# A two-block network on one core: x loaded first, the bonus sums in 16 wide products, and layer 1's last four conditioning vectors moved into the dilated attention

## The chip, the core and the metric

One core of one Trainium2 chip runs the whole program in one launch. The metric is the device time of an execution in microseconds. The two kernels are compared by the median of their runs.

## The reference, cut to what matters

All of it is fp32, for one sequence of S = 256 tokens of width D = 1024. The first block has two layers, RWKV-7 mixing (layer 0) and dilated attention (layer 1), each followed by a hierarchical mixture of experts (MoE). Each layer is modulated by six vectors of 1024 that depend on one conditioning vector c alone:

```python
mod = silu(c) @ ada_w[l] + ada_b[l]          # 1024 x 6144, split in six
shift_a, scale_a, gate_a, shift_m, scale_m, gate_m = split(mod, 6)
x = x + gate_a * mixer(modulate(rms_norm(x), shift_a, scale_a))
x = x + gate_m * moe(modulate(rms_norm(x), shift_m, scale_m))
```

The bonus of the RWKV layer is one number for each token, head and direction, which weighs the token's value: `bonus = sum(r * k_dir * r_k, over the head's 64 channels) * v`. A second block with four more mixers (NSA, stick-breaking, convolution, MoBA) and their MLPs follows; the change does not touch it.

## The kernel before, in words

The program is written for a framework that schedules each engine's instructions and inserts the waits. Weights come through a ring of raw slots of 8 KB a partition: `load` (L317) issues a DMA of 1 MB on SP's queue into the next slot, and SP waits there until the slot is free. Most products are made in three parts of a high and a low half: `split` (L332, L333) has ScalarE write wh, the rounded weights, and VectorE write wl, the rest, in groups of four of 128x512; L361 to L363 are the three products. In the RWKV core the ring has two slots, in the dilated attention six.

`Stream` (L112) runs units of three steps (load, product, end) and issues loads ahead; `staged` (L145) and `weave` interleave units of different kinds, the latter by a string with a letter for each step.

**Conditioning.** `Ada` (L2207) makes the vectors. A vector is four units: a unit loads 128x4x512 of `ada_w` and makes four products (L2239) of a 32-column stationary with silu(c) in one column (`cs`) and 512 moving columns, each in its own 32 partitions. After every second unit VectorE adds the result to the table `am` (L2244). `features` (L2258, L2260) turns a vector into columns by eight products with the selector `asel`, `gate` spreads one over the partitions.

**The order of the program.** The body (L2290) first issues the four units of vector 0, then x (L2325), then those of vector 1, all on SP, and the router's weights of layer 0 (L1248 to L1252: seven small DMAs) before the RWKV layer's own. It normalizes x (L433, L2332), transposes it (L464), and makes vectors 0 and 1, their features, and h (L1674) as x modulated. Seven small DMAs on ScalarE's queue bring the parameter vectors (`vecs`, L494, L500). The other 40 units, the rest of both layers, are a stream that `Rwkv` (L1550) uses as filler: 10 units before the core, 30 in it.

**RWKV.** LoRAs (L1666), k and r projection (`project`, L1631), keys, then for each half: decay rates (L1859), `bonus` (L1800) and `scores` (L1921). In `bonus` VectorE makes the products kq (L1812) and TensorE sums them over a head by 64 products of a 128x64 stationary and two moving columns (L1819); VectorE copies the result (L1823). The core (L1964) runs two chains of four steps each, in pieces that take turns. After three of four turns one fill unit is taken: `if n % 4 < 3: next(fill, None)`.

**After it** come the first MoE (weights through the ring as well), `Dilated` (L1124) with 36 blocks of projection weights ("b"), 16 attention units of several steps ("a": scores, turn, outs) and the output projection ("O", "o"), the second MoE and the second block.

Of the kernel before, what the change touches and what calls it, by code (L numbers as in the profile page):

```python
# [136 lines left out]
def take(g, n):  # L137

    for _ in range(n):
        if next(g, STOP) is STOP:  # L140
            return
        yield

# [118 lines left out]
class Net:  # L262
# [195 lines left out]
    def transposed(self, src, each):  # L458

        for k0 in range(0, 8, 2):  # L460
# [5 lines left out]
            each(k0, ps)  # L466
# [657 lines left out]
class Dilated:  # L1124


    def __init__(self, net, pool, X, w_qkv, w_o, dist, ga):
# [80 lines left out]
        weave("b" * 9 + "babbabbabbabb" * 3 + "Oaaoaoaaa", b=Stream(units), a=staged(16, scores, turn, outs),  # L1208
# [337 lines left out]
ROWY = (0, 64)  # L1546
# [3 lines left out]
class Rwkv:  # L1550
# [10 lines left out]
    def __init__(self, net, xT, G, sh, gate, vec, w, filler, x_src, room, more):  # L1561

        self.net, self.nc, self.tc, self.xT = net, net.nc, net.tc, xT
# [65 lines left out]
    def project(self):  # L1631
# [9 lines left out]
        with net.pool("rp1", "right") as p1:  # L1641
# [83 lines left out]
            with net.pool("rwh", "right", bufs=2) as net.whp, net.pool("rwl", "right", bufs=2) as net.wlp, \  # L1725
# [74 lines left out]
    def bonus(self, pk):  # L1800

        net, nc, v = self.net, self.nc, self.v
        psb = net.w()
        rk = pk.tile([128, 8, 2], F32, name="rkh")
        nc.vector.tensor_tensor(rk, v["rk"][:, 0].unsqueeze(2).to_broadcast([128, 8, 2]),
# [158 lines left out]
    def core(self):  # L1964
# [19 lines left out]
        while chains:  # L1984
            for c in list(chains):
# [7 lines left out]
                if n % 4 < 3:  # L1993
                    next(fill, None)
# [212 lines left out]
class Ada:  # L2207

    def __init__(self, net, pool, cvec, ada_w, ada_b):
# [5 lines left out]
        self.sel = pool.tile([128, 32], F32, name="asel")  # L2217
        nc.vector.tensor_reduce(self.sel, net.ident.rearrange("p (k j) -> p j k", k=4), axis=AX.X, op=ALU.add)
        nc.vector.tensor_tensor(self.sel[:, 0:6], self.sel[:, 0:6], net.ident[:, 8:14], op=ALU.add)
        self.m = [pool.tile([128, 2, 512], F32, name=f"am{l}") for l in range(2)]  # L2220
        for l in range(2):
            nc.gpsimd.memset(self.m[l], 0.0)
            nc.scalar.dma_start(self.m[l][8:14], ada_b[l].rearrange("(v a b) -> v a b", v=6, a=2))
# [283 lines left out]
```

## Time and profile before

| | |
|---|---|
| runs | 2543.34, 2545.49, 2546.83 us (median 2545.49) |
| profiled execution | 2545.04 us, span 2543.3 us |
| mean granted TensorE clock | 0.964 |
| TensorE, weight loads, VectorE, ScalarE busy | 2395.5, 1942.3, 1462.3, 1110.1 us |
| DMA | 547.71 MB, mean 215 GB/s |

The stages that the change touches, in us from the span's start: start and LoRAs 0 to 75, k/r projection 75 to 132, rates, bonus and scores 140 to 205, core 247 to 397, first MoE 457 to 710, dilated attention 717 to 1005.

How to read it: busy time is given for each engine, and a busy TensorE is not TensorE at its peak. An idle stretch counts only if what comes after it is late; so the waits and what ended them matter more than the busy shares. PEclk is the granted TensorE clock as a share of full speed. In the trace an fp32 product has two rows, so that "x8" under TensorE are four products.

### The profile page before, as it was taken

How to read it: one execution, taken by the hardware profiler on the slowest of the kernel's cores; microseconds unless marked ns; L12 is line 12 of the kernel's file. 1: busy time of each engine (PE TensorE's matmuls, PEld its weight loads, DVE VectorE, ACT ScalarE, POOL GpSimd, SP SyncE). 2: the span in 40 equal slices, each digit the busy share in tenths (PEclk: the TensorE clock that was granted, in tenths of full speed). 3: DMA queues.
4: the chain of work that ended last, by engine and by line, in shares of the span. 5: the costliest groups of instructions: out<-in, count | busy, mean ns of one | idle time of the engine just before them, and what ended most of it. 6: DMA issues, size and time to landing. Idle time of an engine off the chain costs nothing. (4 is left out here: it accounts for less than half of the span.)

```text
span 2543.3 us, 41711 instructions
## 1 busy us (share of the span) xinstructions
PE 2395.5 (94%) x17098; PEld 1942.3 (76%) x17098; DVE 1462.3 (57%) x2879; ACT 1110.1 (44%) x2259; POOL 92.3 (4%) x111
## 2 busy tenths in 40 slices
PE   6987888999989999899988999999999899999999
PEld 3855555665579998665557899898999789987998
DVE  4878765443255554433267655566557865577654
ACT  3634233221155553311144544555446654455553
POOL 0000000000000000000022000000000000011000
PEclk9978988999999999899999999999999999999999
DMA  9375888799845444799945255544554245554552
GB/s 309 117 281 199 286 276 318 287 419 412 325 158 173 144 149 156 290 420 400 356 137 195 97 185 182 183 165 149 183 184 147 67 149 182 182 182 133 172 185 74
DMA packets 234077, 547.71 MB, mean 215 GB/s; under 512 B 24810, under 2 KB 75010, under 8 KB 207118
## 3 DMA queue, kind: packets, MB, share of 16 engines
q1 hardware_dynamic: 230774, 532.70, 58.9%
q0 software_dynamic: 1424, 9.44, 1.0%
q8 instruction: 138, 2.26, 0.4%
q10 hardware_dynamic: 1672, 2.74, 0.3%
q14 instruction: 69, 0.57, 0.1%
HBM read 534.36 MB, written 10.49 MB: 214 GB/s over the span
## 5 line engine op out<-in xcount | busy, mean ns | idle before, releaser
L333 DVE TENSOR_TENSOR wl<-raw,wh 128x512 fp32r<-128x512 f32 (+1 forms) x944 | 605.9, 690 | 407.3 <-ACT wh L332 406.2
L332 ACT ACTIVATE wh<-raw 128x512 fp32r<-128x512 f32 (+1 forms) x944 | 530.7, 621 | 506.2 <-issue 214.7
L361 PE MATMUL wk<-xh,wh 128*128 128x256 f32 x1664 | 469.6, 283 | 1.4 <-ACT xh L470 1.3
L362 PE MATMUL wk<-xl,wh 128*128 128x256 f32 x1664 | 469.9, 283 | 0.2 <-DVE xl L472 0.2
L363 PE MATMUL wk<-xh,wl 128*128 128x256 f32 x1664 | 469.7, 283 | 0.0
L361 PEld LDWEIGHTS wk<-xh,wh 128*128 128x128 f32 x1664 | 313.6, 189 | 4.5 <-ACT xh L470 3.0
L362 PEld LDWEIGHTS wk<-xl,wh 128*128 128x128 f32 x1664 | 313.1, 188 | 2.1 <-DVE xl L472 0.5
L363 PEld LDWEIGHTS wk<-xh,wl 128*128 128x128 f32 x1664 | 313.6, 189 | 0.3 <-DVE wl L333 0.3
L1466 PE MATMUL wk<-raw,xg 128*64 128x256 f32 x2048 | 229.4, 381 | 0.0
L1466 PEld LDWEIGHTS wk<-raw,xg 128*64 128x64 f32 x2048 | 144.8, 137 | 80.5 <-issue 11.1
L362 PE MATMUL wk<-wl,hh 128*128 128x512 f32 x512 | 201.4, 393 | 0.0
L361 PE MATMUL wk<-wh,hh 128*128 128x512 f32 x512 | 200.9, 392 | 0.0
L363 PE MATMUL wk<-wh,hl 128*128 128x512 f32 x512 | 199.1, 389 | 0.0
L1472 DVE SCALAR_TENSOR_TENSOR hid<-sg,gs,wk 128x256 f32<-128x256 f32 x32 | 21.4, 668 | 232.1 <-ACT sg L1470 232.1
L1493 PE MATMUL wk<-raw,hidT 128*64 128x512 f32 x512 | 148.4, 598 | 0.0
L361 PE MATMUL wk<-wh,xh 128*128 128x256 f32 (+2 forms) x416 | 141.6, 342 | 1.5 <-ACT xh L470 1.5
L362 PE MATMUL wk<-wl,xh 128*128 128x256 f32 (+2 forms) x416 | 139.3, 335 | 1.7 <-DVE wl L333 1.7
L363 PE MATMUL wk<-wh,xl 128*128 128x256 f32 (+2 forms) x416 | 138.7, 335 | 0.0
L1470 ACT ACTIVATE sg<-wk 128x256 f32<-128x256 f32 x32 | 12.3, 384 | 279.9 <-PE wk L1466 279.9
L363 PEld LDWEIGHTS wk<-wh,hl 128*128 128x128 f32 x512 | 96.1, 188 | 21.7
L361 PEld LDWEIGHTS wk<-wh,hh 128*128 128x128 f32 x512 | 96.2, 188 | 20.9
L362 PEld LDWEIGHTS wk<-wl,hh 128*128 128x128 f32 x512 | 96.2, 188 | 18.6
(491 smaller groups left out, 3873.2 us busy)
## 6 DMA issues: line engine op xcount, KB each, us to landing
raw<-in_moe_w_gate_dram SPq DMA_DIRECT2D x64, 1024.0 KB, 9.4
raw<-in_moe_w_up_dram SPq DMA_DIRECT2D x64, 1024.0 KB, 8.8
raw<-in_moe_w_down_dram SPq DMA_DIRECT2D x64, 1024.0 KB, 8.9
raw<-in_mlp_w_up_dram SPq DMA_DIRECT2D x64, 1024.0 KB, 5.4
raw<-in_mlp_w_down_dram SPq DMA_DIRECT2D x64, 1024.0 KB, 5.2
raw<-in_ada_w_dram SPq DMA_DIRECT2D x45, 1024.0 KB, 7.7
raw<-in_at_w_qkv_dram SPq DMA_DIRECT2D x36, 1024.0 KB, 5.1
raw<-in_sb_w_in_dram SPq DMA_DIRECT2D x12, 1024.0 KB, 5.1
```

Source lines behind the costliest of these rows:

```text
L332: nc.scalar.activation(wh[:, s], raw[:, s], AF.Copy)
L333: self.next_low().tensor_tensor(wl[:, s], raw[:, s], wh[:, s].bitcast(F32), op=ALU.subtract)
L361: mm(out, lh, rh, start=start, stop=False, skip_group_check=True)
L362: mm(out, lh, rl, start=False, stop=False, skip_group_check=True)
L363: mm(out, ll, rh, start=False, stop=stop, skip_group_check=True)
L1466: mm(ps[e * 64:e * 64 + 64, half * 256:half * 256 + 256], xg[:, k, (2 * j + e) * 64:(2 * j + e) * 64 + 64], wts[2 * half + e][:, k], start ...
L1470: nc.scalar.activation(s, ps[:, 0:256], AF.Silu)
L1472: nc.vector.scalar_tensor_tensor(h.rearrange("p f c -> p c f"), s.rearrange("p (c f) -> p c f", f=2), gs, ps[:, 256:512].rearrange("p (c f ...
L1493: mm(ps[e * 64:e * 64 + 64, :], hT[:, f * 128 + e * 64:f * 128 + e * 64 + 64], wts[e][:, f, c * 512:c * 512 + 512], start=f == 0, stop=f = ...
```

## The change

It has four parts. (1) x is loaded by ScalarE's queue as its first DMA; its transposes are made in two pairs between conditioning units, the parameter vectors after them; the router's weights are loaded from within `project`. (2) A conditioning unit loads 128x2x1024 (rows of 4 KB instead of 2 KB); its four products lie in the same 32-partition groups as before, but the two halves of a vector now stand in different partitions of `am`, 512 columns wide; vectors 0 and 1 are added once each. `features` for the MoE (`emod`) has 16 products instead of 8. (3) The bonus takes 16 products with 16 stationary and 256 moving columns, then two ScalarE copies and four transposes. (4) The core's filler holds 24 units instead of 40 and is taken at one turn in three. Vectors 2 to 5 of layer 1 are loaded in `Dilated`, as a stream of 16 units ("m" in the weave); VectorE multiplies them by silu(c) and adds up (`sums`: 64 operations of 128x512), TensorE sums each over the partitions by two products of a one-column selector.

```diff
@@ the body's start
+                nc.scalar.dma_start(x, x_src)
                 nc.sync.dma_start(cst, flat(I['c']).rearrange("(a b) -> a b", b=128))
...
-                    first += [(lambda w=load(): w, prod, end) for load, prod, end in ada.units(0, v)]
-                    if v == 0:
-                        nc.sync.dma_start(x, x_src)
+                    first += [(lambda w=load(): w, prod, end) for load, prod, end in ada.units(0, v, 4)]
...
-                for _ in range(4):
+                for _ in range(3):
                     next(first)
...
-                net.transposed(xn, lambda k0, ps: xT.append((k0, ps)))
+                ts = net.transposes(xn)
+                xT += take2(ts, 2)
+                for _ in range(2):
+                    next(first)
+                xT += take2(ts, 2)
+                next(vecs)
                 trace(first)
-                next(vecs)
...
-            rest = [u for l in range(2) for v in range(2 - 2 * l, 6) for u in rest(l, v)]
-            rest = Stream(rest, 0)
+            fill = Stream([u for l in range(2) for v in range(2 - 2 * l, 6 - 4 * l) for u in rest(l, v)], 0)
...
-            routers.append(weights(0, nc.sync))
...
-            Rwkv(net, xT, scale(0, 0), shift(0, 0), lambda p: ada.gate(p, 0, 2), vec, w, rest, x_src, room, more)
+            Rwkv(net, xT, scale(0, 0), shift(0, 0), lambda p: ada.gate(p, 0, 2), vec, w, fill, x_src, room, more,
+                 lambda: routers.append(weights(0, nc.sync)))
@@ project
                     net.fetch(t, w["rkv"][0], [key])
+                self.later()
@@ bonus
-            for c in range(4):
-                s = c if d == 0 else 3 - c
-                nc.tensor.matmul(psb[ROWY[d]:ROWY[d] + 64, s * 16 + 2 * p:s * 16 + 2 * p + 2],
-                                 q[:, c * 64:c * 64 + 64], rk[:, p], start=(p == 0 and c == 0), stop=True,
-                                 skip_group_check=True)
+            nc.tensor.matmul(psb[:16, d], rk[:, 16 * p:16 * p + 16], q, start=i == 0, stop=p == 7, skip_group_check=True)
         yield from staged(16, product, sums, gap=2)
-        nc.vector.tensor_copy(self.bon, psb[:, :64].rearrange("p (s h) -> p s h", s=4))
+        bt = pk.tile([16, 4, 2, 64], F32, name="bt")
+        for d in range(2):
+            nc.scalar.activation(bt[:, ::1 - 2 * d, d], psb[:16, d].rearrange("p (c t) -> p c t", c=4), AF.Copy)
+        yield
+        ps = net.w()
+        for s in range(4):
+            nc.tensor.transpose(ps[:, s * 16:s * 16 + 16], bt[:, s].rearrange("p d t -> p (d t)"), net.ident[:16, :16])
+        nc.vector.tensor_copy(self.bon, ps[:, :64].rearrange("p (s h) -> p s h", s=4))
@@ core
-                if n % 4 < 3:
+                if n % 3 == 0:
                     next(fill, None)
@@ Dilated
-        weave("b" * 9 + "babbabbabbabb" * 3 + "Oaaoaoaaa", b=Stream(units), a=staged(16, scores, turn, outs),
+        weave("M" + "bbm" * 4 + "b" + "babbmabbmabbabbm" * 3 + "mmmOaaoaoaaa", m=more, b=Stream(units), a=staged(16, scores, turn, outs),
@@ Ada, new
+    def sums(self, pool, l, v):
...
+            def prod(raw):
+                if i == 0:
+                    t.extend(pool.tile([128, 512], F32, name="og", bufs=2) for _ in range(2))
+                for k in range(2):
+                    c = self.cs[:, 2 * i + k, 31:32]
+                    for h in range(2):
+                        r = raw[:, k, h * 512:h * 512 + 512]
+                        if i + k == 0:
+                            nc.vector.tensor_scalar(t[h], r, c, None, op0=ALU.mult)
+                        else:
+                            nc.vector.scalar_tensor_tensor(t[h], r, c, t[h], op0=ALU.mult, op1=ALU.add)
+
+            def end():
+                if i == 3:
+                    ps = net.w()
+                    for h in range(2):
+                        nc.tensor.matmul(ps[32 * h:32 * h + 32], self.one[:, 31 - v:63 - v], t[h],
+                                         start=True, stop=True, skip_group_check=True)
+                    nc.vector.tensor_tensor(self.m[l][0:64], self.m[l][0:64], ps[0:64], op=ALU.add)
```

Where instructions move, three places. First SP's queue at the start of the program (x, raw: the slots that the loads land in), before:

```order
L317 DMA raw<-in_ada_w_dram 128x4x512 x4
L2325 DMA x<-in_x_dram 128x2x1024
L317 DMA raw<-in_ada_w_dram 128x4x512 x4
L1248 DMA rw<-in_moe_router_g_dram 128x8x4
L1250 DMA rw<-in_moe_router_e_dram 128x8x8 x4
...
L1658 DMA x<-in_rw_w_dram 128x8x64 x2
```

and in the changed program:

```order
L322 DMA raw<-in_ada_w_dram 128x2x1024 x8
L1669 DMA x<-in_rw_w_dram 128x8x64 x2
...
L361 DMA raw<-in_rw_w_rkv_dram 128x4x512
L1258 DMA rw<-in_moe_router_g_dram 128x8x4
L1260 DMA rw<-in_moe_router_e_dram 128x8x8 x2
```

x is gone from this queue (it stands first on ScalarE's), and the router's loads stand behind those of the LoRAs and among those of the r weights.

Second, TensorE at the bonus (rkh, kq: its operands; lw: rates; AR, BK: scores; raw, cs: conditioning), before:

```order
L1819 MATMUL wk<-rkh,kq 64x2 x8
L1859 MATMUL wk<-cpack,lw_246 128x128
L1819 MATMUL wk<-rkh,kq 64x2 x4
...
L2239 MATMUL wk<-raw,cs 32x512
L1819 MATMUL wk<-rkh,kq 64x2 x4
L2239 MATMUL wk<-raw,cs 32x512 x3
```

and in the changed program:

```order
L1832 MATMUL wk<-kq,rkh 16x256 x14
L1840 MATMUL wk<-cpack,bt 128x16 x4
L1877 MATMUL wk<-cpack,lw_237 128x128 x4
L2265 MATMUL wk<-raw,cs 32x512 x4
L1877 MATMUL wk<-cpack,lw_238 128x128 x4
L2265 MATMUL wk<-raw,cs 32x512 x4
```

The bonus products stand together, the rate products and the conditioning groups come whole behind them.

Third, VectorE in the dilated attention of the changed program, after its first blocks (og: the running sums of a vector; wl: the splits; dz, dst: an attention step), where before there stood only rows of wl, dz and dst:

```order
L2293 TENSOR_SCALAR og<-raw,cs 128x512 x2
L2295 SCALAR_TENSOR_TENSOR og<-raw,cs,og 128x512 x5
L338 TENSOR_TENSOR wl<-raw,wh 128x512 x4
L2295 SCALAR_TENSOR_TENSOR og<-raw,cs,og 128x512
L338 TENSOR_TENSOR wl<-raw,wh 128x512
L1175 SCALAR_TENSOR_TENSOR dz<-dist,wk 128x256 x3
L338 TENSOR_TENSOR wl<-raw,wh 128x512
L1180 TENSOR_REDUCE dst<-dz 128x1
L338 TENSOR_TENSOR wl<-raw,wh 128x512 x2
L1182 RECIPROCAL dst<-dst 128x1
```

The sums stand before and between the splits of the next weights, one to five in a row.

## Rows read from the trace of the kernel before

**Rows 1.** The page's part 1: busy us, share of the span, instructions.
```profile
PE 2395.5 (94%) x17098; PEld 1942.3 (76%) x17098; DVE 1462.3 (57%) x2879; ACT 1110.1 (44%) x2259; POOL 92.3 (4%) x111
```
**Rows 2.** Windows, start: length, busy us by engine, PEclk, DMA share, GB/s.
```profile
24.00:28.00 4.00, 4.00 (x20) 3.05 (x22) 0.21 (x1) 0.00 (x0) 0.00 (x0) 1.00 1.05 388
28.00:32.00 4.00, 4.00 (x33) 1.59 (x25) 1.14 (x3) 0.00 (x0) 0.00 (x0) 1.00 0.76 86
36.00:40.00 4.00, 0.00 (x0) 0.03 (x1) 3.32 (x8) 3.98 (x9) 0.00 (x0) 0.54 1.14 237
```
**Rows 3.** TensorE's timeline, start: at, us, instructions, [idle before <-releaser].
```profile
23.70 3.65 PE L464 MATMUL wk<-cpack,xn 128*128 128x128 f32 x16 [5.15 <-DVE xn L2332]
27.27 3.84 PE L2239 MATMUL wk<-raw,cs 128*32 128x512 f32 x24
...
32.12 1.06 PE L2239 MATMUL wk<-raw,cs 128*32 128x512 f32 x8
34.00 1.05 PE L2258 MATMUL wk<-asel,am 128*128 128x2 f32 x8 [0.81 <-DVE am L2244]
40.00 1.19 PE L1666 MATMUL wk<-xs,x 128*128 128x256 f32 x2 [4.95 <-DMA w2p<-in_rw_w_dram]
```
**Rows 4.** VectorE's timeline of the start, the same columns.
```profile
22.80 1.42 DVE L2332 TENSOR_SCALAR xn<-x,rstd 128x1024 f32<-128x1024 f32 x2 [0.89 <-POOL rstd L419]
...
33.26 0.69 DVE L2244 TENSOR_TENSOR am<-am,wk 128x512 f32<-128x512 f32 x1 [1.36 <-PE wk L2239]
...
37.54 0.69 DVE L1679 SCALAR_TENSOR_TENSOR xx<-xx,h 128x512 f32<-128x512 f32 x1
```
**Rows 5.** ScalarE's timeline of the start.
```profile
19.16 0.63 ACT L433 ACTIVATE xn<-x 128x512 f32<-128x512 f32 x1 [10.37 <-DMA x<-in_x_dram]
...
35.56 3.76 ACT L1674 ACTIVATE h<-wk,mods 128x256 f32<-128x256 f32 x8 [13.85 <-DVE mods L2351]
```
**Rows 6.** SP's DMA issues of the start (timeline).
```profile
18.32 2.55 SPq L1248 DMA_DIRECT2D rw<-in_moe_router_g_dram  x1
...
32.17 1.00 SPq L1658 DMA_DIRECT2D x<-in_rw_w_dram  x2
```
**Rows 7.** TensorE's groups, 155-182 us: | busy us, mean ns | idle before.
```profile
L1819 PE MATMUL wk<-rkh,kq 128*64 128x2 f32 x128 | 12.1, 234 | 0.6 <-DVE kq L1812 0.6
L2239 PE MATMUL wk<-raw,cs 128*32 128x512 f32 x16 | 7.7, 1060 | 0.0
```
**Rows 8.** Line L1819, bonus products: who waited for it (us, times).
```profile
  DVE kq L1812: 12.0, 6
```
**Rows 9.** Window of the bonus.
```profile
164.00:172.00 8.00, 8.00 (x44) 5.22 (x44) 1.28 (x3) 2.92 (x6) 0.00 (x0) 0.50 0.99 373
```
**Rows 10.** TensorE's costliest group in the core, 236-400 us.
```profile
L2239 PE MATMUL wk<-raw,cs 128*32 128x512 f32 x240 | 41.0, 689 | 15.3 <-DMA raw<-in_ada_w_dram 14.0 <-ACT oT L2183 1.4
```
**Rows 11.** Line L2239, 230-400 us: who waited for it (us, times).
```profile
  DVE am L2244: 27.2, 9
```
**Rows 12.** Windows of k/r projection, core, first MoE and dilated attention.
```profile
80.00:100.00 20.00, 20.00 (x166) 20.00 (x165) 13.65 (x29) 11.21 (x21) 0.00 (x0) 0.98 0.00 1
275.00:320.00 45.00, 38.24 (x752) 25.16 (x750) 32.14 (x84) 13.72 (x30) 2.15 (x4) 0.96 0.96 319
520.00:560.00 40.00, 40.00 (x288) 25.05 (x286) 15.72 (x29) 8.83 (x18) 0.00 (x0) 1.00 1.01 418
760.00:800.00 40.00, 40.00 (x334) 39.69 (x333) 21.21 (x38) 19.20 (x39) 0.00 (x0) 1.00 0.51 166
```
**Rows 13.** TensorE's timeline: wide products, a piece of a conditioning group.
```profile
47.57 3.62 PE L1666 MATMUL wk<-xs,raw 128*128 128x256 f32 x16
...
165.35 1.93 PE L2239 MATMUL wk<-raw,cs 128*32 128x512 f32 x6
```
**Rows 14.** VectorE's timeline in the dilated attention, groups of wl splits.
```profile
741.46 2.50 DVE L333 TENSOR_TENSOR wl<-raw,wh 128x512 fp32r<-128x512 f32 x4 [3.11 <-ACT wh L332]
746.68 0.69 DVE L333 TENSOR_TENSOR wl<-raw,wh 128x512 fp32r<-128x512 f32 x1 [2.71 <-ACT wh L332]
```

More of the change, by code (lines that the diff above doesn't have):

```diff
@@ L142, in take, with take2 @@
         yield
+def take2(g, n):
+    return [next(g) for _ in range(n)]
 def staged(n, *stages, gap=1, at=None):
@@ L458, in transposed, with transposes @@
     def transposed(self, src, each):
+        for k0, ps in self.transposes(src):
+            each(k0, ps)
+    def transposes(self, src):
         for k0 in range(0, 8, 2):
@@ L2216, in __init__ @@
         nc.scalar.activation(self.cs[:, :, 31], cvec, AF.Silu)
[L2217 to L2220, printed above, removed]
+        self.one = pool.tile([128, 63], F32, name="aone")
+        nc.gpsimd.memset(self.one, 0.0)
@@ L2221, in __init__ @@
+        nc.gpsimd.memset(self.one[:, 31:32], 1.0)
+        self.sel = pool.tile([128, 2, 32], F32, name="asel")
+        nc.vector.tensor_reduce(self.sel, net.ident.rearrange("p (k h j) -> p h j k", k=2, h=2), axis=AX.X, op=ALU.add)
+        self.m = [pool.tile([128, 2 - l, 512], F32, name=f"am{l}")[:, 0] for l in range(2)]
         for l in range(2):
             nc.gpsimd.memset(self.m[l], 0.0)
-            nc.scalar.dma_start(self.m[l][8:14], ada_b[l].rearrange("(v a b) -> v a b", v=6, a=2))
@@ L2225, in units, with unit @@
-    def units(self, l, v):
+        for h in range(2):
+            nc.vector.tensor_tensor(self.sel[:, h, 0:6], self.sel[:, h, 0:6], net.ident[:, 8 + 32 * h:14 + 32 * h], op=ALU.add)
+            for l in range(2):
+                nc.scalar.dma_start(self.m[l][8 + 32 * h:14 + 32 * h],
+                                    ada_b[l].rearrange("(v a b) -> v a b", v=6, a=2)[:, h])
+    def units(self, l, v, n=2):
         net, nc = self.net, self.net.nc
-        def unit(hb, k0, ps):
+        def unit(i, ps):
@@ L2242, in end @@
             def end():
-                if k0:
-                    nc.vector.tensor_tensor(self.m[l][:, hb], self.m[l][:, hb], ps[0], op=ALU.add)
+                if i % n == n - 1:
+                    nc.vector.tensor_tensor(self.m[l], self.m[l], ps[-1], op=ALU.add)
             return load, prod, end
-        out = []
-        for hb in range(2):
-            ps = []
-            out += [unit(hb, k0, ps) for k0 in (0, 4)]
-        return out
-    def features(self, l, v, n, out, order="p (k c) -> p k c"):
+        ps = []
@@ L2254, in features @@
+    def features(self, l, v, n, out, by_p=False):
         net, nc = self.net, self.net.nc
         pf = net.w()
-        m = self.m[l].rearrange("p a b -> p (a b)").rearrange(order, k=8)
         for j in range(8):
-            nc.tensor.matmul(pf[:, j * n:j * n + n], m[:, j],
-                             self.sel[:, v:v + n], start=j == 0, stop=True, skip_group_check=True)
+            for h in range(2) if by_p else (j // 4,):
+                m = self.m[l][:, j::8] if by_p else self.m[l][:, j % 4 * 128:j % 4 * 128 + 128]
+                nc.tensor.matmul(pf[64 * h:64 * h + 64, j * n:j * n + n] if by_p else pf[:, j * n:j * n + n], m,
+                                 self.sel[:, h, v:v + n], start=j == 0, stop=True, skip_group_check=True)
```

56 lines of the change are left out of this document (36 added, 20 removed).

## The prediction

> **What bounds the kernel now.** I read the busy table first: TensorE is busy for 94% of the span and VectorE for 57% [rows 1]. Such an average hides stages with different limits, so I then read windows of the four stages that the change touches, and in each what the late engine waited for.
>
> *Start.* From 24 to 28 us the DMA engines are full (share 1.05, 388 GB/s), and right after that the rate falls to 86 GB/s [rows 2]. So the eight loads of conditioning weights and x, 9 MB, have landed by about 28.0 us. TensorE's timeline shows what is late: the transposes of the normalized x and three groups of conditioning products stand before the last one, at 32.12, and the feature products follow at 34.00 [rows 3]; VectorE's add between them is at 33.26 [rows 4]. ScalarE's first h row starts at 35.56, after 13.85 us in which it had nothing to do [rows 5]. The LoRA products wait 4.95 us for a weight, until 40.00 [rows 3]: SP took the router's many small loads from 18.32 on, and came to the first LoRA load at 32.17 [rows 6]. From 36 to 40 TensorE does nothing, and the granted clock is 0.54 [rows 2].
>
> *Bonus.* The 64 small products of the bonus are TensorE's largest group between 155 and 182 us, 12.1 us, with 7.7 us of conditioning products between them [rows 7]. VectorE waits for the small products six times, 12.0 us in all [rows 8]. From 164 to 172 TensorE is busy for all 8.00 us, at a granted clock of 0.50 [rows 9].
>
> *RWKV core.* Thirty conditioning units (four 512-wide products each) run as fill between the steps of the two chains: 41.0 us of TensorE, and 15.3 us of idle time ahead of them, 14.0 of it for the load of their weights [rows 10]. VectorE, which carries much of the chains, waits 27.2 us for their results, in 9 waits [rows 11]. The DMA share is 0.96 in 275 to 320, though only 319 GB/s move [rows 12].
>
> *After the core.* The first MoE is bound by its loads (share 1.01, 418 GB/s [rows 12]), and their buffers are those that the core frees, so what the core gains should reach the end. The dilated attention is bound by TensorE: 40.00 of 40 us, VectorE 21.21, DMA share 0.51 [rows 12].
>
> **The change, part by part.** The profiled execution took 2545.04 us; the median of the runs is 2545.49, 0.45 above, so the sum holds for both.
>
> 1. *Start.* x goes first, on ScalarE's queue. Its squares, its scaling and its transposes then run while the eight loads still arrive, and the router's loads go behind the LoRA's. The bytes are the same, so I leave the last conditioning load at 28.0. After it come one group of products (1.06 [rows 3]), one add (0.69 [rows 4]), and from the start of the feature products to that of h as much as now, 35.56 − 34.00 = 1.56 [rows 3, 5]. With 0.1 for the hand-overs, h starts at 28.0 + 1.06 + 0.69 + 1.56 + 0.1 = 31.4 instead of 35.56: −4. The LoRA weights, issued up to 14 us earlier [rows 6], are no longer last. Bounds: −2, when two units are left at 28.0 and the small parameter loads, now behind x, make the features late; −7, when most of the LoRA's wait of 4.95 goes as well. The router's loads now take SP's time ahead of the k/r projection; the DMA engines have a share of 0.00 in 80 to 100 [rows 12], so I put them at 0. Were SP late, the next weights of that projection would be late next.
>
> 2. *Bonus.* Out go 12.1 us of small products. In come 16 products of 16x256. The nearest row is a 128x256 product: 16 rows, which are 8 products, in 3.62 us [rows 13], 0.45 each, so 7.2 at full clock. The four transposes cost at most 0.9 (3.65 for 16 [rows 3]), and two ScalarE copies of 256 columns 0.8 (two thirds each of the 0.63 for 512 columns [rows 5]). The small products also cut two conditioning groups in pieces: such a piece alone took 1.93 at half clock [rows 13], and both groups 7.7 [rows 7]; whole, they take 2.1 at full clock [rows 3] or 3.9 at half. Sum at full clock: −12.1 + 7.2 + 0.9 + 0.8 − 5.6 = −8.8. At half clock: −12.1 + 14.4 + 1.8 + 0.8 − 3.8 = +1.1. The profile shows TensorE busy here for all 8.00 us and the clock at 0.50 all the same [rows 9], so a busy row does not promise the full clock. The Trainium skill (TensorE: Matmul & The Clock Gate, "What's actually happening") says that the clock is throttled by default and that the engine's activity releases it; by that rule the stretch, filled with products before and after, would run at full clock, and its term would be −8.8. The row above does not bear that out. I take −5, in the upper half towards the full clock, because the two-column products were most of the stretch at half clock, and they are what goes. The end of the bonus is on the path: the scores of the second half wait for what VectorE makes after it.
>
> 3. *Core.* The fill shrinks from 30 units to 14, one step in three. Sixteen units take 16/30 of 41.0 us with them, 21.9 us of TensorE, and the 15.3 us of waits should all but vanish, since 14 MB in 150 us are 40 us of full DMA. Not all of the 21.9 was on the path of the chains. Bounds: −14 (only the waits for loads) and −37 (all of both). VectorE's 27.2 us [rows 11] are a second reading of the same loss, and I take −28: the waits and three fifths of the products. Eight of 15 adds (0.69 each) leave VectorE too; they are in this.
>
> 4. *Dilated attention.* Sixteen loads of 1 MB come in. At 2.7 us each (388 GB/s [rows 2]) they raise the DMA share from 0.51 to about 0.68, and hide. VectorE gets 64 operations of 128x512: 56 with two tensor inputs at 0.69, and 8 scalings at 0.36 (a scaling of 1024 columns is 0.71; [rows 4]): 42 us. It has 19 of 40 us free over some 250 us, so there is room in sum. In place, a unit of four is 2.75 us, and idle gaps of 2.7 to 3.1 us stand before the groups of wl splits [rows 14], so a unit just fits. On TensorE there are two 512-wide products for each of four vectors, half a group or 0.53 us, and eight feature products that moved here from the core (1.05 [rows 3]): about 3. For units that don't fit I add 2: together +5. Bounds: 0, and +48, a rival below.
>
> 5. *Feature products.* Sixteen instead of eight for the MoE's shift and scale, in both layers: at most +1, half of a group's 1.05 each.
>
> Sum: −4 − 5 − 28 + 5 + 1 = −31, or 2514 us.
>
> **The rivals.**
> *The core is bound by its chains.* If the products were hidden and only the waits go, the core gives −14: 2528. For it: VectorE is busy for 32.14 of the 45 us in 275 to 320. Against: TensorE is busier, 38.24 [rows 12].
> *The clock falls in the core.* With fewer fills TensorE does less, and where it stood still, at 36 to 40, the clock was halved [rows 2]. At 38.24 of 45 us it works some 136 us in 160; less 22 that is 114. If a tenth of it goes from 1.06 to 1.93 [rows 3, 13], 9 us come back: 2523. Against: in 275 to 320 the granted clock is 0.96 with waits in it [rows 12].
> *The start keeps its time,* because another load is last (a small parameter load behind x, or x and the first loads in each other's way). That is 0 in place of −4: 2518. For it: a share of 1.05 leaves no room [rows 2]. Against: transposes, not bytes, stood before the last group.
> *VectorE delays TensorE in the dilated attention (slower).* VectorE works in order, so a unit that waits for its load, or sits ahead of a wl group whose turn on TensorE has come, holds it up. If each of 16 units costs its whole 2.75 us there, that is 44, and with the products 48 in place of +5: −36 + 48 = +12, or 2557. It decides from the point at which the gap before the wl groups is shorter than a unit. For it: the gap is hardly longer [rows 14], and the order puts up to five of the operations in a row before four wl splits. Against: VectorE is idle for almost half of the stage.
>
> **How the numbers follow.** My forecast has 0.50, the chain-bound core 0.17, the clock 0.11, the unchanged start 0.09, and VectorE in the attention 0.13. Of the last, 0.09 is slower by over 0.2% (5 us, about what a measurement of this kernel can tell from no change) and 0.04 within it, when two thirds of the units stall. So faster 0.87, same 0.04, slower 0.09. The forecast's own range is 2501 to 2526: core −37 and bonus −8.8 below, core −22 and the bonus at half clock above. The whole range reaches to the chain-bound core with 10 us more in the attention, 2538, and below to 2498, when the start is at its best end too: 8 in 10.
>
> **What would show it.** h starts near 31.4; the bonus ends some 5 us earlier than the start's gain alone explains; in the core the conditioning products wait under 4 us for loads, and the core is 28 us shorter; the first MoE lasts as long as before; in the attention TensorE stays at 39 or 40 of 40 us, and the stage grows by 5 us. I am wrong if TensorE waits for wl there, if the chains take the same time with the waits gone, or if the granted clock in the core falls clearly below 0.9.

## The result, and the profile after

The changed kernel takes 2507.32 us (2506.80 to 2511.17, four runs) against 2544.41 us (2538.54 to 2546.83, four runs): a ratio of 0.9854, 95% interval 0.9836 to 0.9872, some 37 us faster. The profiled execution of the changed kernel took 2511.17 us, the longest of its four, so its trace shows 33.9 us of the 37 (34.2 of the span).

The trace says where. The table gives the length of each stage in the two traces: the start up to the first product of the scores, from there to the first row of the inverse on VectorE, from there to the first expert product (inverse, core, output projection, routing), the first MoE, the dilated attention from its first projection product to its last gated sum, and the rest.

| stage | before | after | difference | predicted |
|---|---|---|---|---|
| start, k and r projection | 143.1 | 140.5 | −2.6 | −4 |
| scores and bonus | 73.5 | 58.9 | −14.6 | −5 |
| inverse, core, output | 240.8 | 216.3 | −24.5 | −28 |
| first MoE | 264.2 | 264.4 | +0.2 | 0 |
| dilated attention | 284.9 | 295.0 | +10.1 | +5 |
| the rest | 1536.8 | 1534.0 | −2.8 | +1 |

The sum of busy times, beside [rows 1], tells little of this. TensorE lost 32 us and VectorE gained as many:

```profile
PE 2363.0 (94%) x16926; PEld 1926.9 (77%) x16926; DVE 1494.5 (60%) x2939; ACT 1109.5 (44%) x2261; POOL 91.6 (4%) x113
```

**The start.** Windows, with the columns of [rows 2]:

```profile
24.00:28.00 4.00, 2.66 (x22) 0.69 (x20) 0.46 (x2) 0.00 (x0) 0.00 (x0) 1.00 1.03 389
28.00:32.00 4.00, 1.94 (x8) 0.20 (x8) 0.69 (x1) 0.00 (x0) 0.00 (x0) 0.63 1.22 221
32.00:36.00 4.00, 3.58 (x16) 3.49 (x16) 0.33 (x2) 0.00 (x0) 0.00 (x0) 0.50 1.08 217
```

TensorE's timeline of the changed kernel, beside [rows 3]:

```profile
20.65 1.83 PE L473 MATMUL wk<-cpack,xn 128*128 128x128 f32 x8
...
26.59 1.07 PE L2265 MATMUL wk<-raw,cs 128*32 128x512 f32 x8 [0.99 <-DMA raw<-in_ada_w_dram]
29.28 1.94 PE L2265 MATMUL wk<-raw,cs 128*32 128x512 f32 x8 [1.62 <-DMA raw<-in_ada_w_dram]
32.03 3.58 PE L2315 MATMUL wk<-asel,am 128*128 128x2 f32 x16 [0.81 <-DVE am L2271]
40.54 1.19 PE L1677 MATMUL wk<-xs,x 128*128 128x256 f32 x2 [4.94 <-issue]
```

and ScalarE's, beside [rows 5]:

```profile
14.78 0.63 ACT L438 ACTIVATE xn<-x 128x512 f32<-128x512 f32 x1
...
36.11 3.75 ACT L1685 ACTIVATE h<-wk,mods 128x256 f32<-128x256 f32 x8 [18.77 <-DVE mods L2411]
```

x is used at 14.78 instead of 19.16, and the transposes are done by 24.5. But h does not start earlier: 36.11 against 35.56. The last group comes at 29.28, in 1.94 us, and the feature products take 3.58. TensorE waits between the last groups, and the granted clock falls to 0.63 and then 0.50, where before the transposes kept it busy and the clock at 1.00 [rows 2, 3]. The first LoRA product follows the first h row by 4.4 us in both kernels (35.56 and 40.00 before, 36.11 and 40.54 after), and in every other trace of this document. So it was h that held the LoRAs up, and not the weight named in [rows 3]: the loads of w2p are now issued at 30.0 and 31.2 instead of 36.0 and 37.1, and the 4.4 us stay.

**The bonus.** TensorE's groups from 153 to 182 us, beside [rows 7]:

```profile
L1832 PE MATMUL wk<-kq,rkh 128*16 128x256 f32 x32 | 8.0, 395 | 0.3 <-DVE kq L1827 0.3
L1877 PE MATMUL wk<-cpack,lw 128*128 128x128 f32 x32 | 4.9, 291 | 0.0
L2265 PE MATMUL wk<-raw,cs 128*32 128x512 f32 x16 | 2.1, 604 | 0.0
```

from the view of line L1832, what the new products waited for (us, times), where before VectorE waited for them [rows 8]:

```profile
  DVE kq L1827: 1.3, 3
```

and two windows, beside [rows 9]:

```profile
164.00:172.00 8.00, 6.56 (x53) 4.17 (x52) 4.75 (x9) 3.81 (x13) 0.00 (x0) 1.00 0.93 362
172.00:180.00 8.00, 6.19 (x76) 5.28 (x72) 8.00 (x14) 2.11 (x6) 1.10 (x2) 1.00 0.33 121
```

The bonus products fall from 12.1 to 8.0 us, the two conditioning groups from 7.7 to 2.1, twice as many rate products take 4.9 (16 rows took 4.6 in the window before), and from 164 us on the granted clock is 1.00 where it was 0.50. The products wait 1.3 us for VectorE, instead of VectorE waiting 12.0 us for them.

**The core.** The conditioning products in it, beside [rows 10], and who waits for them, beside [rows 11]:

```profile
L2265 PE MATMUL wk<-raw,cs 128*32 128x512 f32 x112 | 18.9, 672 | 0.0
```

```profile
  DVE am L2271: 6.6, 2
```

41.0 us of products and 15.3 of idle time have become 18.9 and none; VectorE waits 6.6 us for them instead of 27.2. The chains, from their first product to the start of their last, take 113.9 us (230.3 to 344.2) instead of 142.2 (247.5 to 389.7). What TensorE waits for most in the core is now the chains' own VectorE work (the waits of TensorE, 228 to 346 us):

```profile
PE wk L2085 <- DVE QT L1979: 7.2, 1, 7.2
PE wk L2196 <- DVE gy L2192: 6.9, 2, 3.7
```

**The dilated attention.** Windows, beside [rows 12], TensorE's new groups, and VectorE's:

```profile
720.00:760.00 40.00, 40.00 (x324) 38.71 (x324) 29.20 (x52) 19.17 (x38) 0.00 (x0) 1.00 0.83 267
760.00:800.00 40.00, 40.00 (x311) 38.37 (x310) 21.80 (x40) 21.39 (x43) 0.00 (x0) 1.00 0.56 184
800.00:840.00 40.00, 40.00 (x309) 38.20 (x308) 28.36 (x53) 19.21 (x39) 0.00 (x0) 1.00 0.57 185
```

```profile
L2301 PE MATMUL wk<-og,aone 128*32 128x512 f32 x16 | 4.2, 604 | 0.0
...
L2315 PE MATMUL wk<-asel,am 128*128 128x2 f32 x16 | 1.9, 250 | 1.1 <-DVE am L2303 1.1
```

```profile
L2295 DVE SCALAR_TENSOR_TENSOR og<-raw,cs,og 128x512 f32<-128x512 f32 x56 | 39.5, 744 | 6.7 <-DMA raw<-in_ada_w_dram 6.7
...
L2293 DVE TENSOR_SCALAR og<-raw,cs 128x512 f32<-128x512 f32 x8 | 3.6, 478 | 0.3 <-DMA raw<-in_ada_w_dram 0.3
```

TensorE stays at 40.00 of 40 us. VectorE goes to 22 to 29 us, and waits for DMA 6.7 us in the sums. The products over partitions take 4.2 us, twice what was put down, the feature products 1.9 and 1.1 of waiting.

### The profile page after: what moved, and what is told of

It is laid out like the page before. It is cut to its first block, busy times and chain, and to the rows that moved or that the text cites. A ratio compares the mean times of both kernels' runs of the same rounds, so it can differ in the third digit from the quotient of the medians.

```text
span 2509.1 us, 41426 instructions
## 1 busy us (share of the span) xinstructions
PE 2363.0 (94%) x16926; PEld 1926.9 (77%) x16926; DVE 1494.5 (60%) x2939; ACT 1109.5 (44%) x2261; POOL 91.6 (4%) x113
## 3 DMA queue, kind: packets, MB, share of 16 engines
q1 hardware_dynamic: 218214, 531.65, 59.1%
## 4 chain that ended last, share of the span: by engine, by line
PE 42%; DVE 5%; POOL 1%; ACT 1%; issue 1%; POOLq 0%; ACTq 0%
PE wk L366 13%; PE wk L367 13%; PE wk L368 13%; DVE cv L1098 2%; DVE wl L338 1%; POOL qr L424 1%; PE wk L1094 0%; PE wk L776 0%; PE wk L232 0%; PE wk L953 0%; DVE qa L728 0%; PE wk L777 0%; DVE qss L723 0%; PE wk L768 0%; DVE qa L716 0%
## 5 line engine op out<-in xcount | busy, mean ns | idle before, releaser
L1476 PEld LDWEIGHTS wk<-raw,xg 128*64 128x64 f32 x2048 | 144.6, 137 | 80.7 <-issue 11.1
L368 PEld LDWEIGHTS wk<-wh,hl 128*128 128x128 f32 x512 | 96.1, 188 | 21.7
```

Source lines behind the costliest of these rows:

```text
L368: mm(out, ll, rh, start=False, stop=stop, skip_group_check=True)
L1476: mm(ps[e * 64:e * 64 + 64, half * 256:half * 256 + 256], xg[:, k, (2 * j + e) * 64:(2 * j + e) * 64 + 64], wts[2 * half + e][:, k], start ...
```

## Experiments

Each ran beside the kernel before on the same chip; its ratio is to that. e5 and e6 are edits of the kernel before, the others of the changed one. The last two columns come from each trace: scores to inverse, and inverse to first expert.

| run | median us | ratio (95%) | scores, bonus | core |
|---|---|---|---|---|
| changed kernel | 2507.32 | 0.9854 (0.9836, 0.9872) | 58.9 | 216.3 |
| e1 start undone | 2510.25 | 0.9856 (0.9835, 0.9876) | 58.5 | 215.8 |
| e2 bonus undone | 2516.89 | 0.9881 (0.9862, 0.9900) | 72.9 | 212.0 |
| e3 all 40 units in the core | 2527.32 | 0.9931 (0.9914, 0.9949) | 59.6 | 238.0 |
| e4 three turns in four | 2519.80 | 0.9895 (0.9876, 0.9914) | 59.4 | 230.2 |
| e5 before, new bonus only | 2533.43 | 0.9947 (0.9934, 0.9960) | 59.2 | 242.9 |
| e6 before, wide products added | 2553.62 | 1.0032 (1.0015, 1.0049) | 77.5 | 248.3 |
| e7 the moved vectors by TensorE | 2522.71 | 0.9907 (0.9893, 0.9920) | 59.1 | 211.5 |
| e8 VectorE's additions left out | 2506.42 | 0.9835 (0.9821, 0.9848) | 58.8 | 214.3 |
| e9 start kept busy | 2506.44 | 0.9846 (0.9830, 0.9861) | 58.8 | 212.4 |
| e10 one turn in four | 2523.98 | 0.9919 (0.9904, 0.9934) | 59.0 | 226.2 |
| e11 e4, features later | 2516.71 | 0.9878 (0.9861, 0.9895) | 58.8 | 223.4 |
| e12 features later | 2512.15 | 0.9873 (0.9855, 0.9891) | 58.7 | 219.1 |

The kernels were not all measured together, and the median of the kernel before was 2544.41 to 2547.93 us beside them. A difference of two medians of less than some 4 us therefore says little, and below the ratios are given beside the medians where they differ.

The core's column shows how far one trace repeats: six kernels with the same core (the changed one, e1, e2, e7, e8, e9) have 211.5 to 216.3 us there. The changed kernel's own trace is at the upper end of that.

**e1: the start undone.**

```diff
-                nc.scalar.dma_start(x, x_src)
...
+                    if v == 0:
+                        nc.sync.dma_start(x, x_src)
...
+            routers.append(weights(0, nc.sync))
```

(with the transposes, the parameter vectors and the units in the old order)

> The changed kernel with its start undone: x on SP's queue after the fourth conditioning load, all transposes before the last units, the router's loads ahead of the LoRA's. Theory A (the start gives next to nothing: h starts at 36.1 against 35.6 in the two traces, because TensorE idles once the transposes are out of its way and runs the last group and all eight feature products at half clock; only some 2 to 3 us come later, from loads that are no longer behind the router's): 2507 + 2 to 3, so 2509 to 2511, first k product at about 75.5 again. Theory B (the -4 of the prediction is in the total): 2511 to 2513. Theory C (the start costs, the later gain comes from elsewhere): 2506 or less.

The medians are 2.9 us apart and the ratios 0.0002, so the total does not tell the two kernels apart. The trace does, a little: h at 36.3, the first k product at 77.2 and the scores at 144.6, against 36.1, 73.7 and 140.5. Theory A holds in its place, not in the total: x first brings h no earlier. What comes later is a matter of the order on VectorE. In e1 (VectorE, ScalarE, TensorE):

```profile
70.75 4.91 DVE L338 TENSOR_TENSOR wl<-kd,wh 128x512 fp32r<-128x512 f32 x8 [1.22 <-ACT wh L337]
...
76.49 0.63 ACT L479 ACTIVATE sh<-xs 128x512 fp32r<-128x512 f32 x1 [0.87 <-DVE xs L1660]
...
77.17 0.38 PE L366 MATMUL wk<-sh,wh 128*128 128x256 f32 x1 [1.45 <-ACT sh L479]
```

and in the changed kernel (VectorE):

```profile
69.07 2.50 DVE L338 TENSOR_TENSOR wl<-kd,wh 128x512 fp32r<-128x512 f32 x4 [1.22 <-ACT wh L337]
```

The first k product needs sh, which ScalarE makes of VectorE's xs; and VectorE makes xs behind eight wl splits in e1 (and before: the product starts at 75.49, after 1.45 us of the same wait) but behind four in the changed kernel, where it starts at 73.69. That the router's loads are the reason, as the expectation had it, was not tried by itself.

**e9: TensorE kept busy at the start.**

```diff
+                warm = net.w()
+                for n in (0, 2, 1):
+                    for _ in range(n):
+                        nc.tensor.matmul(warm, net.ident, xn[:, 0, 0:512], start=True, stop=True, skip_group_check=True)
+                    next(first)
                 trace(first)
```

> The changed kernel with three 512-wide products of no use put between the last three conditioning groups, where TensorE idles for 1.0 and 1.6 us. Theory A (x first gains nothing because TensorE, idle once the transposes are early, drops to 0.50 and runs the last group in 1.94 and the feature products in 3.58): the granted clock stays at 0.9 or more until 32 us, the last group takes 1.06 and the features about 1.9, h starts at 33.3 to 33.8 and the first LoRA product some 2 us earlier; total 2 us less, at the edge of what can be measured. Theory B (the loads bound the start): h stays at 36, or comes later by the added products.

Theory A holds. The window, and TensorE's timeline:

```profile
28.00:32.00 4.00, 3.19 (x26) 1.27 (x25) 0.69 (x1) 0.00 (x0) 0.00 (x0) 1.00 1.27 225
```

```profile
28.17 2.07 PE L2265 MATMUL wk<-raw,cs 128*32 128x512 f32 x16
31.05 1.99 PE L2315 MATMUL wk<-asel,am 128*128 128x2 f32 x16 [0.81 <-DVE am L2271]
```

The clock stays at 1.00 through 32 us, two groups take 2.07 together, the features 1.99, h starts at 33.5 and the first LoRA product at 37.98 instead of 40.54. In the total it is 2506.44 against 2507.32, which the intervals don't tell apart.

One trace of e9 would not be enough, for the fall of the clock varies. Nine traces have the same start without the added products. In six the granted clock of 28 to 32 us is 0.51 to 0.64, the last group takes 1.94, the features 3.58, and h starts at 35.9 to 36.1. In e7 and e12 the clock falls only behind the last group (1.07), and the features take 2.86 and 3.57 (h at 34.3 and 35.0). In e11 it stays, by itself, and its rows are those of e9, with h at 33.6:

```profile
29.30 1.06 PE L2265 MATMUL wk<-raw,cs 128*32 128x512 f32 x8 [1.62 <-DMA raw<-in_ada_w_dram]
31.18 1.95 PE L2315 MATMUL wk<-asel,am 128*128 128x2 f32 x16 [0.81 <-DVE am L2271]
```

h goes with the clock in all ten, while the last group starts at 29.0 to 29.3 in all. So the half clock held the start back by some 2.5 us: 0.9 in the group and 1.6 in the features. That the added products hold the clock up is likely, but e9 was profiled once, and e11 has the full clock without them.

**e2 and e5: the bonus undone in the new kernel, and alone in the old one.** In both the whole of `bonus` is exchanged, in e2 as the minus lines, in e5 as the plus lines:

```diff
-                nc.tensor.matmul(psb[ROWY[d]:ROWY[d] + 64, s * 16 + 2 * p:s * 16 + 2 * p + 2],
-                                 q[:, c * 64:c * 64 + 64], rk[:, p], start=(p == 0 and c == 0), stop=True,
+            nc.tensor.matmul(psb[:16, d], rk[:, 16 * p:16 * p + 16], q, start=i == 0, stop=p == 7, skip_group_check=True)
```

> The changed kernel with the bonus of the kernel before (64 products of two columns). Theory A (the bonus part is worth what the two traces show between the start of the scores and the first row of the inverse, 17.2 minus 2.6, about 14 us, through the granted clock and through VectorE no longer waiting 12 us): 2507 + 12 to 15, so 2519 to 2522, granted clock 0.50 again for some 15 us. Theory B (the term of the prediction, 5): 2512. If the rest of the 14 us belongs to the conditioning units' new shape or to the start, the time stays under 2514.

> The kernel before with the bonus of the changed kernel and nothing else. Theory A (the bonus part stands on its own: the stretch from the first scores to the inverse is 14 to 16 us shorter, and the rest shifts with it): 2545 - 13, so 2530 to 2534; granted clock 1.00 in 160 to 180. Theory B (it pays only together with the rest, since the core is bound by loads whose time does not shift): 2538 or more.

In the traces the stage is 72.9 us in e2 and 59.2 in e5, so the bonus part is worth 14 us in either direction. In e5 the total falls by as much, 14.5 us of the medians (ratio 0.9947), and theory A holds. In e2 the median rises by 9.6 us (6.9 by the ratios), less than was expected by theory A and more than by theory B, with runs from 2509 to 2526 us. The profiled run is the longest of them and has the lowest mean granted clock, 0.961; the shortest has the highest, 0.970. That the price of the old bonus differs from run to run with the clock would fit, but the other runs have no trace, and it is not shown.

**e6: wide products among the narrow ones.**

```diff
+        dump = net.w()
...
+            nc.tensor.matmul(dump[:, :256], net.ident, q, start=True, stop=True, skip_group_check=True)
```

> The kernel before with one wide product (128x128 stationary, 256 moving columns, result not read) put behind each group of four two-column products of the bonus: 16 products of 0.45 us at full clock, 7.2 us more of TensorE. Theory A (the two-column products leave the clock at 0.50, wide ones lift it): granted clock 0.9 or more in 160 to 182, a piece of a conditioning group 1.06 instead of 1.93, and the scores end no later than before (201.7, within 2) although work was added. Theory B (the clock is not the reason; TensorE's order and work are): the scores end 7 to 14 us later.

Theory A falls as it was put. TensorE's timeline, and three windows:

```profile
164.62 0.63 PE L1820 MATMUL wk<-rkh,kq 128*64 128x2 f32 x8
165.18 1.02 PE L1823 MATMUL wk<-kq,cpack 128*128 128x256 f32 x2
166.12 1.02 PE L1820 MATMUL wk<-rkh,kq 128*64 128x2 f32 x8
...
186.25 1.94 PE L2241 MATMUL wk<-raw,cs 128*32 128x512 f32 x8
...
189.76 1.07 PE L2241 MATMUL wk<-raw,cs 128*32 128x512 f32 x8
```

```profile
156.00:164.00 8.00, 8.00 (x85) 6.22 (x83) 6.32 (x13) 7.86 (x13) 0.00 (x0) 1.00 1.01 415
172.00:180.00 8.00, 8.00 (x41) 5.59 (x40) 1.70 (x4) 0.00 (x0) 0.00 (x0) 0.50 0.01 3
180.00:188.00 8.00, 8.00 (x36) 4.71 (x35) 0.75 (x2) 1.62 (x7) 0.00 (x0) 0.50 0.00 0
```

The clock falls to half at about 165 us although every second row there is a 128x128x256 product, and TensorE is busy for all 8.00 us of the windows. It is back at the second conditioning group behind the narrow products (1.94, then 1.07). So wide products beside the narrow ones did not lift the clock here; in e5, without the narrow ones, it is 1.00 from 156 to 180 us. The scores end at 204.1, 2.4 us later than before, though 16.2 us of products were added: the scheduler now puts the conditioning groups behind the bonus, whole, at 1.94 and 1.07 instead of 7.7 us in pieces. That the pieces were dear was a term of the prediction, and this agrees with it.

**e3 and e4: the core's filler.**

```diff
e3
-                if n % 3 == 0:
+                if n % 4 < 3:
...
-            fill = Stream([u for l in range(2) for v in range(2 - 2 * l, 6 - 4 * l) for u in rest(l, v)], 0)
+            fill = Stream([u for l in range(2) for v in range(2 - 2 * l, 6) for u in rest(l, v)], 0)
...
-        weave("M" + "bbm" * 4 + "b" + "babbmabbmabbabbm" * 3 + "mmmOaaoaoaaa", m=more, b=Stream(units), a=staged(16, scores, turn, outs),
+        weave("b" * 9 + "babbabbabbabb" * 3 + "Oaaoaoaaa", b=Stream(units), a=staged(16, scores, turn, outs),
...
-                        Stream([u for v in range(2, 6) for u in rest(1, v, dp)]))
+                        None)
e4
-                if n % 3 == 0:
+                if n % 4 < 3:
```

> The changed kernel with all 40 units as filler, three turns in four, and nothing of them in the dilated attention (the units keep their rows of 4 KB). Theory A (the core pays 25 us for 16 more units and their loads, the attention pays 8 for having them): 2507 + 17, so 2521 to 2527, waits of the conditioning products for loads 10 us or more. Theory B (rows of 4 KB remove most of the waits by themselves): under 2516.

> The changed kernel with the filler taken at three turns in four, as before, with its 24 units. Theory A (in the core VectorE and the chains are the bound once the number of units is down, the rate hardly matters): 2507, within 3. Theory B (what counts is the spacing: units that follow closely wait for the two slots): 2512 to 2518, with waits of the products for loads of 5 us or more.

e3 holds to theory A: the core is 21.7 us longer, the attention 7.5 shorter (287.5), the median 20 higher (2527.32, just above the range that was expected). Its rows of 4 KB still wait for loads (TensorE's conditioning group in the core):

```profile
L2265 PE MATMUL wk<-raw,cs 128*32 128x512 f32 x240 | 39.4, 678 | 11.8 <-DMA raw<-in_ada_w_dram 10.4 <-ACT oT L2201 1.4
```

e4 goes to theory B, against my own: the rate alone costs 12.5 us of the medians (10 by the ratios), with the same 24 units. Two things come with it. At its start the feature products stand in TensorE's queue ahead of the first products of the chains, and wait for an add that VectorE has behind the inverse; the chains start at 238.5 instead of 230.3:

```profile
235.07 3.54 PE L2315 MATMUL wk<-asel,am 128*128 128x2 f32 x16 [8.12 <-DVE prod L1973]
```

and later the products wait for loads again (from 236 us on):

```profile
L2265 PE MATMUL wk<-raw,cs 128*32 128x512 f32 x96 | 14.7, 643 | 10.8 <-DMA raw<-in_ada_w_dram 10.1 <-ACT oT L2201 0.7
```

So of the 20 us between e3 and the changed kernel, 12.5 are the rate, and some 7.5, net of the attention's price, are the 16 units. The second part rests on the medians alone: in the two traces the 16 units cost the core 7.8 us (238.0 against 230.2) and the attention 7.6 (295.1 against 287.5), and both spans are 2522.7; the profiled run is the shortest of e3 and the longest of e4. All 40 units at one turn in three were not tried, so what the move to the attention brings beside the slower rate stays open.

**e11 and e12: the feature products four units later,** at the fast and at the slow rate.

```diff
-                if v in (1, 4):
+                if v in ((1, 4) if l else (1, 5)):
```

> The kernel with three turns in four (24 units), but with the feature products of layer 0's fifth vector called four units later, after its sixth. Theory A (at the fast rate the core starts 8.2 us later because the feature products stand in TensorE's queue ahead of the first products of the chains and wait 8.1 us for an add that VectorE has behind the inverse): the first product of the chains starts at 230 to 232 again, total 2519.8 - 8, so 2510 to 2513. Theory B (another wait takes its place there, the next conditioning add): still 236 or later, and 2517 or more.

> The changed kernel (one turn in three) with the same feature products called four units later. Theory A (at the slow rate they fit into a gap in which TensorE waits 7.2 us for the inverse anyway): no difference, 2507 within 3. Theory B (they cost there too): 2502 to 2504.

In e11 the chains start at 227.68, so the wait of 8 us was the reason for that part (theory A in its place, not in its total):

```profile
227.68 3.63 PE L2085 MATMUL wk<-Xs,QT 32*32 32x64 f32 x127 [3.19 <-DVE QT L1979]
...
239.88 1.93 PE L2265 MATMUL wk<-raw,cs 128*32 128x512 f32 x8 [4.22 <-DMA raw<-in_ada_w_dram]
```

The stage is 6.8 us shorter than in e4, and the median 3 us lower (4 by the ratios), about half of the 8 or less: the next wait for a load stands at 239.88. In e12 the stage is 219.1, 2.8 above the highest of the same core, and the median 4.8 higher; the intervals overlap, so no gain, and perhaps a loss. The feature products stood well where they were.

**e10: one turn in four.**

```diff
-                if n % 3 == 0:
+                if n % 4 == 0:
```

> The changed kernel with the filler taken at one turn in four instead of three. Theory A (the rate matters through the place of the first units and through the waits for loads; at one in three both are gone, and what remains is the chains): the core stays as it is or is 1 to 3 us longer, because more units are left for its end; 2506 to 2511. Theory B (each unit taken inside costs the chains its whole time): 3 to 5 us less.

Both theories fall: 16.7 us slower. The chains are hardly faster (112.4 us from their first product to their last, against 113.9), and four units are left over behind them:

```profile
359.18 3.63 PE L2265 MATMUL wk<-raw,cs 128*32 128x512 f32 x16
368.54 1.93 PE L2265 MATMUL wk<-raw,cs 128*32 128x512 f32 x8 [5.73 <-DMA raw<-in_ada_w_dram]
...
373.77 1.95 PE L2315 MATMUL wk<-asel,am 128*128 128x2 f32 x16 [0.81 <-DVE am L2271]
```

They stand in TensorE's queue ahead of the output projection and wait for loads (5.73), their groups run at half clock (1.93), and the projection starts at 375.6 instead of 362.6. A filler that is too slow costs as much as one that is too fast.

**e7 and e8: who pays in the attention.** e7 gives the moved vectors back to TensorE, e8 leaves out VectorE's 56 additions.

```diff
e7
-                        Stream([u for v in range(2, 6) for u in rest(1, v, dp)]))
+                        Stream([u for v in range(2, 6) for u in rest(1, v)]))
e8
-                        else:
-                            nc.vector.scalar_tensor_tensor(t[h], r, c, t[h], op0=ALU.mult, op1=ALU.add)
```

> The changed kernel with layer 1's last four vectors made by TensorE in the dilated attention: 16 units of four products, 1.06 us each, 17.0 us, in place of VectorE's 64 operations and of 8 products on TensorE (4.2 us). Theory A (the attention is bound by TensorE and VectorE's 42 us are hidden): 12 to 14 us more in the attention, 2519 to 2521. Theory B (VectorE's sums delay TensorE there, and make the 8 us by which the stage grew): 2507 to 2512.

> The changed kernel without the 56 additions of VectorE's sums in the dilated attention (each vector is only its first scaled block, so layer 1's last four vectors are incomplete); the 16 loads, 8 scalings, and all products on TensorE stay. Theory A (the stage grew by 8 us through TensorE's own products: 4.2 for the sums over partitions, 1.9 for the feature products, 1.1 of waiting for them): nothing changes, 2507 within 2, the stage again 295 us. Theory B (VectorE): 5 to 8 us less, 2499 to 2502.

e7: the attention takes 312.2 us, 17.2 more, and the median is 15.4 higher (13.5 by the ratios); the group of its 64 products:

```profile
L2265 PE MATMUL wk<-raw,cs 128*32 128x512 f32 x128 | 16.4, 602 | 0.0
```

They cost 12.2 us more than the 4.2 of the sums. The rest lies in the attention's own steps: TensorE waits 4.8 us for dz instead of 2.0, and the products of the scores (wk<-dk,dq) and the transposes of dz (wk<-cpack,dz) take 40.2 us instead of 37.5.

e8: the attention takes 293.3 us, 1.7 less, the median 0.9 less, and VectorE is back near the 21.21 of [rows 12]:

```profile
800.00:840.00 40.00, 40.00 (x309) 38.20 (x309) 22.57 (x42) 19.55 (x40) 0.00 (x0) 1.00 0.67 219
```

Theory A holds in both, in the stage. By the ratios e8 is 5 us faster, with intervals that overlap, so its total alone does not exclude theory B. Of the 10 us by which the stage grew, 1.7 are VectorE's additions (3.4 against the longest of the eight traces with the same attention, 295.0 to 296.7); 7.2 are TensorE's new products and their one wait. Some 1 us is neither, and e3, with nothing of the moved work there, takes 287.5 against 284.9 before. So VectorE's sums are all but hidden, and cost less than the same sums on TensorE by 14 to 17 us.

## Why the prediction was right, and where its terms were not

The time is inside the range and 7 us from the forecast. That it came so near is in part luck. In the traces the terms are off by +1.4 (start), −9.6 (bonus), +3.5 (core), +5.1 (attention) and −3.8 us (the rest), and these cancel to some −3. The three large terms have the right sign and in the main the right mechanism; the start gained its part by another way.

*Start (−4).* The failed step is "from the start of the feature products to that of h as much as now", together with the last group at full clock. I read what the transposes delayed, and not that they kept TensorE's clock up; with them gone early, the last group and all the feature products ran at half clock (1.94 and 3.58), and h came no earlier. I had also overlooked that half of the feature products were already done before, at 31.21, since the two halves of a vector were added at different times; now all wait for the last add. The ten traces at e9 show that the half clock makes 2.5 of the 4.7 us by which h missed 31.4; the rest is the last load, used at 29.3 and not at 28.0, and the features, 2.0 us and not 1.05 even at full clock. The 2.6 us that the stage gained come after the LoRAs began. That the LoRAs waited for a weight was a misreading: they follow h by 4.4 us with the weight late or early, so nothing of the 4.95 could go.

*Bonus (−5, measured −14.6).* The step that failed is the choice between the two clocks. My term at full clock, −8.8, was the nearer, and it still left out the rate products between the small ones and the scores behind them, which also ran at half clock before, and VectorE's 12.0 us of waiting [rows 8], which I had read and not used. e5 and e2 show the size in the stage, 14 us; how it divides between the clock, the pieces and the waits was not separated. The rule of the Trainium skill that I had weighed (TensorE: Matmul & The Clock Gate, "What's actually happening") does not describe this stretch if busy rows are taken for the activity that it means: in e6 TensorE is busy for all 8.00 us of 172 to 180, at 0.50.

*Core (−28, measured −24.5, and 25 to 29 in other traces of the same core).* The size was right. The chains alone are 28.3 us shorter, and what stands between them and the output projection is 3 us longer (18.4 against 15.4). But the working put it all on the number of units, and e4 shows that half of it or more is the rate: with the same units at three turns in four the core is 14 us longer. The rival in which the core is bound by its chains (2528) did not come, nor the one with the clock: while the chains run, it is 0.89 (230 to 344 us) against 0.88 before (247 to 390). The sign of a clock clearly below 0.9 was set too high, from one stretch at 0.96.

*Attention (+5, measured +10).* The mechanism held: the stage grew through TensorE's products and not through VectorE. The two products over partitions of a vector cost 1.05 us and not 0.53: two products took as long as a whole group of four (1.06). The eight feature products took 1.9 us, with 1.1 of waiting before them; the 1.05 that I had put down is the time of four (a product has two rows). The 2 for units that don't fit had no row to stand on, and e8 shows 1.7 to 3.4 in its place. The additions took 744 ns and not 690, the scalings 478 and not 360; that was hidden too. The slower rival did not come, as e8 shows: without the additions the stage is hardly shorter. The additions went into the gaps before the wl splits. VectorE's wait for ScalarE there, in the stage before (717 to 1007 us) and now (676 to 975):

```profile
DVE wl L333 <- ACT wh L332: 109.5, 58, 3.9
```

```profile
DVE wl L338 <- ACT wh L337: 72.4, 42, 3.2
```

with TensorE still at 40.00 of 40.

*Feature products (+1).* The sign was wrong. TensorE's rows for the MoE's features in layer 0, before and after:

```profile
430.49 3.74 PE L2258 MATMUL wk<-asel,am 128*128 128x2 f32 x16
```

```profile
388.44 2.09 PE L2315 MATMUL wk<-asel,am 128*64 128x2 f32 x32
```

The sixteen products take 2.09 us where the eight took 3.74, at a granted clock of 1.00 in both; layer 1 has the same times, at 1006.32 before and at 975.01 after. I had taken the 1.05 of other feature products for them. Why the eight took longer was not tried, and the total does not show the gain: the rest of the program varies by 4 us between kernels that are equal there (1532.2 to 1536.5).

## What to carry to other kernels

Filler work in an engine's queue has a right rate and not only a right amount: too fast, it stood ahead of the critical work here and waited for loads or for another engine (e4); too slow, what was left over stood ahead of the next stage (e10). Work that seems to delay an engine may be what keeps its clock: before moving it away, ask what the engine does in its place. And sums of weights against one vector cost little on a VectorE that waits half of its time beside a bound TensorE: here some 2 to 3 us of 295, against 17 on TensorE.

## What the runs showed that was not expected

TensorE stood at half clock in stretches of products with two moving columns while the profile showed it busy for 8.00 of 8 us, and a 128x256 product after each group of four of them did not bring the clock back (e6). A conditioning group of four products took 1.06 us whole, and 3.85 us at half clock (1.92 and 1.93) when one of its products was issued apart from the other three, against 1.94 whole. The moment at which the clock fell behind the waits of the start, 0.9 to 1.6 us long, differed between traces of the same code: the features took 1.95 (e11), 2.86 (e7) or 3.58 us.
